# A transposed-map pair of the second group takes one of the scores' two PSUM banks

## The chip, the core and the metric

The kernel runs on one core of a Trainium2 chip. The metric is the device time of one execution in microseconds. The profile shows one execution of the program; its times are from the profiled span's start, and the engines are PE (TensorE matmul; its weight loads are a row of their own, PEld), DVE (VectorE), ACT (ScalarE) and SP, which here only issues DMAs.

## What is computed

One layer on a sequence of 1024 tokens of width 2048, in float32. An adaptive norm, one input projection, then two mixers side by side and one output projection with residual and final norm:

```
proj = hn @ w_in
# group A: 8 heads; two softmax maps per head, subtracted, chunk-causal over blocks of 128 queries
p = softmax(where(mask, q k^T * scale, -inf));  a = p[:, 0] - lam * p[:, 1];  o = a @ v
# group B: 4 heads; a state per chunk of 64 tokens
state = decay * state + k_dec^T @ v;  o = q @ state
mixed = concat([rmsnorm(o_A) * silu(dg), rmsnorm(o_B) * silu(gg)]) @ w_out
out = rmsnorm(x + gate * mixed)
```

## The kernel before

Tokens are worked on in two halves of 512. Every large product runs as three matmuls on a high and a low part of its operands (lines 189 to 192 and 218 to 220), so PE has 11118 matmuls. A `unit` (line 821) is a quarter of a half: two attention heads h0 and h1 and one gated-linear head. In the program's order a unit has: the projections dk, dq, dg of h0, the projection of v for both heads (`make_v`, line 605), attention of h0, the projections of h1, attention of h1, then gq, two gg and gv, and `gla` (line 773). The second half has the same four units with twice the keys, and the output projection of the first half follows (lines 1007 to 1056).

The engines' instructions are not issued in the program's order. A planner simulates the program and lets each engine take, of what is ready, what comes first in the program's order. What it decides is fixed: at run time every engine works through its list in that order. So while attention waits for a softmax, PE's list holds matmuls of a projection that comes later in the program; below these are called filler.

PSUM has eight banks of 128x512 fp32. Three pools hold them: `pj_p` has four, for projections (`pb`, `pa`); `sc_p` has two, for the scores `s` of attention (line 663) and the two state products `kv` of a gla step (line 785); `ms_p` has two, for the transposed maps `tp` (line 700), the attention output `av` (line 696), the sums of the norm `nps` (line 624), the gla output `o` (line 802) and some small things.

Attention of a head works on two groups of two query blocks. For each block there are two maps, each of one piece (first half) or two pieces (second half: `ka`, the 512 keys of the first half, and `kb`). A piece is scored into a bank of `sc_p`, its maximum is taken on DVE (line 669), and ACT writes the exponentials to a buffer `p` (line 678; six buffers). The two maps are then subtracted (line 693). When a group's two blocks are done, the maps are transposed, two key blocks at a time, into a `tp` tile (line 708), split into a high part on ACT and a low part on DVE (`aT`, line 711, two buffers) and multiplied with v into `av` (lines 720 to 722). The second group has two `tp` tiles per head in the first half and four in the second half. `av` keeps its bank of `ms_p` through its group, so the `tp` tiles of the group take the other bank in turn.

In `gla`, a step t multiplies `kd_z` and `gv` into two `kv` banks (line 788), adds them to the state `S` on DVE (line 796, two buffers), splits the state (`sr`, one buffer) and multiplies it with gq into `o` (line 804). `gv` shares the three `vb` buffers with the v of two heads (lines 606 and 877).

Of the kernel before, what the change touches and what calls it, by code (L numbers as in the profile page):

```python
# [10 lines left out]
F32 = mybir.dt.float32  # L11
# [8 lines left out]
P = 128  # L20
# [3 lines left out]
TOK = 512  # L24
# [71 lines left out]
def body(ctx, tc, A, out):  # L96
# [13 lines left out]
    sc_p = ctx.enter_context(tc.tile_pool(name="sc", bufs=2, space=PSUM))  # L110
    ms_p = ctx.enter_context(tc.tile_pool(name="ms", bufs=2, space=PSUM))
# [116 lines left out]
    def split(hi, lo, src, lo_eng=None):  # L228
        SC.copy(hi, src)
        (lo_eng or V).tensor_tensor(lo, src, hi.bitcast(F32), ALU.subtract)  # L230
# [412 lines left out]
    def attention(half, h, qt, kb, vb, g_t):  # L643
# [8 lines left out]
        for grp in range(2):  # L652
# [44 lines left out]
            nk = nka + 2 * grp + 2  # L697
            for k0 in range(0, nk, 2):
                last = k0 == nk - 2
                tp = ms_p.tile([P, TOK], F32, name=f"tp{half}{h}{grp}{k0}", tag="ms")  # L700
                pi, ko = (0, k0) if k0 < nka else (half, k0 - nka)
                spans = []
                o = 0
                for k in (0, 1):
                    for bi in range(2):
                        if last and k == 1 and bi == 0:
                            continue
                        PE.transpose(tp[:, o:o + P], at[bi][pi][:, (ko + k) * P:(ko + k + 1) * P], ident)
                        o += P
                aT = hd_p.tile([P, 2, TOK], F32R, name=f"aT{half}{h}{grp}{k0}", tag="aT", bufs=2)  # L710
                split(aT[:, 0, :o], aT[:, 1, :o], tp[:, :o])
                for k in (0, 1):
                    vv, kt = (va, k0 + k) if k0 < nka else (vb, ko + k)
                    vh, vl = vv[:, kt, 0, :], vv[:, kt, 1, :]
                    if last and k == 1:
                        dst, sl = av[:, P:2 * P], slice(2 * P, 3 * P)
                    else:
                        dst, sl = av[:, :2 * P], slice(k * 2 * P, (k + 1) * 2 * P)
                    first = k0 == 0 and k == 0
                    PE.matmul(dst, vh, aT[:, 0, sl], start=first, stop=False, skip_group_check=True)  # L720
                    PE.matmul(dst, vh, aT[:, 1, sl], start=False, stop=False, skip_group_check=True)
                    PE.matmul(dst, vl, aT[:, 0, sl], start=False, stop=last and k == 1, skip_group_check=True)
# [98 lines left out]
    def unit(half, g, first, kdec):  # L821
# [23 lines left out]
        g0 = gate_tile(h0)  # L845
        vt = make_v(dv_ps if first else proj_a(A["wina"][A_AT[("dv", g)]], hn), half, g)
        attention(half, h0, qt0, kb0, vt[0], g0)
        kb1 = make_k(src("dk", h1), half, h1)
        qt1 = make_q(src("dq", h1), half, h1)
        g1 = gate_tile(h1)  # L850
        attention(half, h1, qt1, kb1, vt[1], g1)
        if g == 0:
            kdec = gla_p.tile([P, 4, 512], F32, name=f"kdec{half}", tag="kdec")
# [254 lines left out]
```

## Time and profile before

| | before |
|---|---|
| median of 3 runs | 1957.07 us (1956.12 to 1958.6) |
| the profiled execution | 1955.52 us |
| its span | 1953.7 us |
| PE busy in the span | 1905.5 us (98%) |
| DVE, ACT busy | 1321.9 us, 968.7 us |
| mean granted TensorE clock | 0.987 of 2.4 GHz |

The span runs from the first to the last instruction; 1.8 us of the execution's time lie around it. Matmuls overlap, and a matmul's duration in a row is longer than the distance to the next one's start, so the time a run of matmuls takes is read from starts. A bracket at the end of a timeline row gives the idle time of that engine just before the instruction, and which instruction ended it.

### The profile page before, as it was taken

How to read it: one execution, taken by the hardware profiler on the slowest of the kernel's cores; microseconds unless marked ns; L12 is line 12 of the kernel's file. 1: busy time of each engine (PE TensorE's matmuls, PEld its weight loads, DVE VectorE, ACT ScalarE, POOL GpSimd, SP SyncE). 2: the span in 40 equal slices, each digit the busy share in tenths (PEclk: the TensorE clock that was granted, in tenths of full speed). 3: DMA queues.
4: the chain of work that ended last, by engine and by line, in shares of the span. 5: the costliest groups of instructions: out<-in, count | busy, mean ns of one | idle time of the engine just before them, and what ended most of it. 6: DMA issues, size and time to landing. Idle time of an engine off the chain costs nothing.

```text
span 1953.7 us, 28965 instructions
## 1 busy us (share of the span) xinstructions
PE 1905.5 (98%) x11118; PEld 1677.0 (86%) x11118; DVE 1321.9 (68%) x2496; ACT 968.7 (50%) x1811; POOL 0.7 (0%) x6
## 2 busy tenths in 40 slices
PE   7999999999989999999999999999999999899998
PEld 4888999899868989889899898989888998688888
DVE  7897876577779767656676666866785675534444
ACT  4222865566545566545545555554654544323323
POOL 0000000000000000000000000000000000000000
PEclk9899999999999999999999999999999999799999
DMA  9884434332665444433344323533263723466543
GB/s 362 294 290 136 155 125 141 119 106 87 209 210 166 136 138 150 135 89 101 97 154 117 106 91 108 162 111 99 87 198 117 267 86 106 167 239 213 162 150 120
DMA packets 111758, 298.16 MB, mean 153 GB/s; under 512 B 11098, under 2 KB 31322, under 8 KB 111108
## 3 DMA queue, kind: packets, MB, share of 16 engines
q1 hardware_dynamic: 111620, 296.32, 46.6%
q8 instruction: 87, 1.43, 0.3%
q14 instruction: 51, 0.42, 0.1%
HBM read 258.00 MB, written 38.28 MB: 152 GB/s over the span
## 4 chain that ended last, share of the span: by engine, by line
PE 86%; DMA 6%; DVE 6%; issue 1%; ACT 1%; SPq 0%; DVEq 0%; ACTq 0%
PE pa L218 8%; PE pa L220 8%; PE pa L219 8%; PE pa L1051 4%; PE pa L1052 4%; PE pa L1053 4%; PE pb_dk L190 2%; PE pb_dk L191 2%; PE pb_dk L192 2%; PE pb_gg L190 2%; PE pb_dg L191 2%; PE pb_dq L192 2%; PE pb_dq L191 2%; PE pb_dq L190 2%; PE pb_dg L192 2%; PE pb_gg L192 2%
## 5 line engine op out<-in xcount | busy, mean ns | idle before, releaser
L180 DVE TENSOR_TENSOR w<-wr,w 128x1024 fp32r<-128x1024 f32 (+1 forms) x294 | 352.1, 1198 | 276.0 <-ACT w L179 274.8
L179 ACT CAST w<-wr 128x1024 fp32r<-128x1024 f32 (+1 forms) x294 | 303.2, 1031 | 431.2 <-PE pa L1053 116.1
L220 PE MATMUL pa<-w,hn 128*128 128x256 f32 (+1 forms) x1152 | 328.2, 285 | 0.0
L218 PE MATMUL pa<-w,hn 128*128 128x256 f32 (+1 forms) x1152 | 327.7, 285 | 0.0
L219 PE MATMUL pa<-w,hn 128*128 128x256 f32 (+1 forms) x1152 | 327.7, 285 | 0.0
L219 PEld LDWEIGHTS pa<-w,hn 128*128 128x128 f32 x1152 | 219.6, 191 | 2.4 <-issue 0.2
L218 PEld LDWEIGHTS pa<-w,hn 128*128 128x128 f32 x1152 | 219.5, 191 | 2.3 <-issue 0.5
L220 PEld LDWEIGHTS pa<-w,hn 128*128 128x128 f32 x1152 | 219.5, 191 | 1.5 <-issue 0.2
L678 ACT ACTIVATE p<-s,sm 128x512 f32<-128x512 f32 (+2 forms) x192 | 110.7, 580 | 130.1 <-DVE sm L675 59.0
L1051 PE MATMUL pa<-w,mx 128*128 128x512 f32 x384 | 150.7, 392 | 0.4 <-DVE h L996 0.4
L1052 PE MATMUL pa<-w,mx 128*128 128x512 f32 x384 | 150.4, 392 | 0.0
L1053 PE MATMUL pa<-w,mx 128*128 128x512 f32 x384 | 149.9, 392 | 0.0
L669 DVE TENSOR_REDUCE sm<-s 128x1 f32<-128x512 f32 (+2 forms) x192 | 105.5, 551 | 46.7 <-PE s L666 44.1
L190 PE MATMUL pb_gg<-hn,w 128*128 128x512 f32 x224 | 88.1, 394 | 0.6 <-DVE vb L230 0.6
L191 PE MATMUL pb_dk<-hn,w 128*128 128x512 f32 x224 | 88.1, 393 | 0.0
L190 PE MATMUL pb_dk<-hn,w 128*128 128x512 f32 x224 | 88.1, 393 | 0.0
L190 PE MATMUL pb_dg<-hn,w 128*128 128x512 f32 x224 | 88.1, 393 | 0.0
L191 PE MATMUL pb_gg<-hn,w 128*128 128x512 f32 x224 | 88.0, 393 | 0.0
L192 PE MATMUL pb_dq<-hn,w 128*128 128x512 f32 x224 | 87.9, 392 | 0.0
L191 PE MATMUL pb_dg<-hn,w 128*128 128x512 f32 x224 | 87.8, 392 | 0.0
L192 PE MATMUL pb_gg<-hn,w 128*128 128x512 f32 x224 | 87.8, 392 | 0.0
L192 PE MATMUL pb_dk<-hn,w 128*128 128x512 f32 x224 | 87.6, 391 | 0.0
(394 smaller groups left out, 4376.9 us busy)
## 6 DMA issues: line engine op xcount, KB each, us to landing
wr<-in_winb SPq DMA_DIRECT2D x142, 512.0 KB, 3.8
wr<-in_wina SPq DMA_DIRECT2D x72, 512.0 KB, 3.8
wr<-in_wout SPq DMA_DIRECT2D x64, 512.0 KB, 3.5
ada<-in_wada SPq DMA_DIRECT2D x44, 512.0 KB, 5.0
stage<-in_wgate SPq DMA_DIRECT2D x64, 256.0 KB, 3.0
mx<-mixd SPq DMA_DIRECT2D x32, 512.0 KB, 8.1
ada_kdec<-in_wada SPq DMA_DIRECT2D x20, 512.0 KB, 6.6
mixd<-wr_d SPq DMA_DIRECT2D x16, 512.0 KB, 4.5
```

The source lines that it names most:

```text
L179: paced = SC.copy(w[:, 0, :n], raw[:, :n])
L180: (lo_eng or V).tensor_tensor(w[:, 1, :n], raw[:, :n], w[:, 0, :n].bitcast(F32), ALU.subtract)
L190: PE.matmul(ps, w_hi, h[:, 0, :], start=first, stop=False)
L191: PE.matmul(ps, w_hi, h[:, 1, :], start=False, stop=False)
L192: PE.matmul(ps, w_lo, h[:, 0, :], start=False, stop=last)
L218: PE.matmul(o, ah, wh, start=st, stop=False, skip_group_check=True)
L219: PE.matmul(o, ah, wl, start=False, stop=False, skip_group_check=True)
L220: PE.matmul(o, al, wh, start=False, stop=kt == KT - 1, skip_group_check=True)
L678: SC.activation(p_[:, :n], pss[pi][:, :n], AF.Exp, bias=nm, scale=0.125, accum_out=sm[:, 4 + 2 * m_ + pi:5 + 2 * m_ + pi])
L1051: PE.matmul(pss[t_], ah, wh, start=kt == 0, stop=False)
L1052: PE.matmul(pss[t_], ah, wl, start=False, stop=False)
L1053: PE.matmul(pss[t_], al, wh, start=False, stop=kt == KT - 1)
```

## The change

The `tp` tiles of a head's second group (`grp` is 1) come from `sc_p` with its tag instead of `ms_p`. The first group's stay where they were. No instruction is added or removed; 48 of the 80 `tp` tiles have another bank.

```diff
-                tp = ms_p.tile([P, TOK], F32, name=f"tp{half}{h}{grp}{k0}", tag="ms")
+                tp = (sc_p if grp else ms_p).tile([P, TOK], F32, name=f"tp{half}{h}{grp}{k0}", tag="sc" if grp else "ms")
```

## Rows read from the trace of the kernel before

**Rows 1.** The page's part 1: busy time, share of span, instructions.

```profile
PE 1905.5 (98%) x11118; PEld 1677.0 (86%) x11118; DVE 1321.9 (68%) x2496; ACT 968.7 (50%) x1811; POOL 0.7 (0%) x6
```

**Rows 2.** Stretches: us, PE, PEld, DVE, ACT, POOL busy (count), clock, DMA share, GB/s.

```profile
1450.00:1500.00 50.00, 48.01 (x239) 40.23 (x238) 30.01 (x51) 23.46 (x40) 0.00 (x0) 1.00 0.40 124
1500.00:1550.00 50.00, 46.51 (x331) 44.56 (x330) 34.98 (x76) 28.27 (x61) 0.00 (x0) 0.93 0.72 266
...
1650.00:1700.00 50.00, 39.88 (x156) 29.98 (x156) 35.49 (x68) 21.54 (x55) 0.00 (x0) 0.80 0.50 173
```

**Rows 3.** Waits of PE: us in total, times, longest.

```profile
PE s L665 <- ACT p L678: 4.6, 5, 1.9
...
PE av L720 <- ACT aT L229: 2.9, 2, 2.6
```

**Rows 4.** The tile aT: durations min/median/max ns, first and last start, forms.

```profile
L229 ACT CAST aT<-tp x80: 455/577/651, 233.6 to 1659.9; 128x512 fp32r<-128x512 f32 x48, 128x384 fp32r<-128x384 f32 x32
L230 DVE TENSOR_TENSOR aT<-tp,aT x80: 494/676/693, 234.1 to 1661.3; 128x512 fp32r<-128x512 f32 x48, 128x384 fp32r<-128x384 f32 x32
```

**Rows 5.** Timeline of PE, the last head's second group: start, us, instruction.

```profile
1643.50 0.60 PE L708 MATMUL tp<-ident,p 128*128 128x128 f32 x4
...
1650.30 0.60 PE L708 MATMUL tp<-ident,p 128*128 128x128 f32 x4
...
1657.28 0.49 PE L708 MATMUL tp<-ident,p 128*128 128x128 f32 x3
1660.39 0.38 PE L720 MATMUL av<-aT,vb 128*128 128x256 f32 x1 [2.63 <-ACT aT L229]
```

**Rows 6.** Timeline of DVE and PE around norm sums, first and last head end.

```profile
272.31 0.39 PE L628 MATMUL nps_d<-wr_d,ones 128*128 128x512 f32 x1
272.55 0.49 PE L708 MATMUL tp<-ident,p 128*128 128x128 f32 x3
...
1635.75 0.69 DVE L230 TENSOR_TENSOR sr<-S,sr 128x512 fp32r<-128x512 f32 x1 [0.69 <-ACT sr L229]
...
1665.09 0.80 PE L628 MATMUL nps_d<-wr_d,ones 128*128 128x512 f32 x1 [1.84 <-ACT wr_d L229]
1665.68 1.48 PE L804 MATMUL o<-sr,gq 128*128 128x512 f32 x3
```

**Rows 7.** Timeline of PE, end of one head, first scores of the next.

```profile
1559.83 0.40 PE L665 MATMUL s<-ka,qt 128*128 128x512 f32 x1
...
1566.49 0.40 PE L665 MATMUL s<-ka,qt 128*128 128x512 f32 x1
...
1571.24 0.49 PE L708 MATMUL tp<-ident,p 128*128 128x128 f32 x3
...
1587.58 0.49 PE L708 MATMUL tp<-ident,p 128*128 128x128 f32 x3
```

**Rows 8.** Timeline of PE and ACT, state products before the last unit's v.

```profile
1457.24 0.88 PE L788 MATMUL kv<-gv,kd_z 128*128 128x256 f32 x6
...
1474.35 0.39 PE L192 MATMUL pb_gq<-hn,w 128*128 128x512 f32 x1
...
1476.01 0.60 PE L788 MATMUL kv<-gv,kd_z 128*128 128x256 f32 x3
1476.77 0.66 ACT L229 CAST vb<-pa 128x256 fp32r<-128x256 f32 x2
1479.03 0.49 PE L708 MATMUL tp<-ident,p 128*128 128x128 f32 x3
1480.17 0.50 PE L190 MATMUL pb_gg<-hn,w 128*128 128x512 f32 x1 [0.65 <-DVE vb L230]
```

**Rows 9.** Timeline of PE and DVE at the end of attention.

```profile
1655.65 0.39 PE L1053 MATMUL pa<-w,mx 128*128 128x512 f32 x1
...
1677.12 1.88 DVE L996 TENSOR_TENSOR h<-pa,gbs 128x512 f32<-128x512 f32 x3
1677.86 0.80 PE L1051 MATMUL pa<-w,mx 128*128 128x512 f32 x1 [0.45 <-DVE h L996]
```

## The prediction

> **What bounds the kernel now.** The page's part 1 comes first. PE is busy 1905.5 of 1953.7 us [rows 1], so all of PE's idle time is 48.2 us, and a change that adds and removes no instruction can win at most that, plus time lost at the lower clock level. Then the stretches, 50 us each, to see where the idle time lies. A good part of it is outside attention (the start, the last stores). What the change can touch is in three stretches of the second half [rows 2]: 2.0 us (50 less 48.01) in 1450:1500, 3.5 us in 1500:1550 and 10.1 us in 1650:1700, where the granted clock is also 0.80. Everywhere else in the second half's attention filler covers the waits: PE waited 2.9 us in all for a split map and 4.6 us in all for an exponential to leave a scores' bank [rows 3]. So attention's length matters only through what runs out of filler. The timelines tell which: in 1650:1700 the filler's last matmul is at 1655.65 and the next is at 1677.86, after DVE has emptied a bank [rows 9]; around 1475 the last gq matmul is at 1474.35, and the next projection waits until 1480.17 for DVE's split of v [rows 8].
>
> **Banks are handed out in the program's order.** This is the reading on which my forecast rests. The step-0 state of the last gla is split by 1636.4 (1635.75 and 0.69), yet the `o` made from it starts at 1665.68, right behind `nps` of the last head at 1665.09; in the first head, the next head's first transposes start at 272.55, right behind `nps` at 272.31 [rows 6]. Both are users of `ms_p` that come later in the program than `nps`, and one bank of the pool had been free for some time. I take it that a pool's tiles get their banks in the program's order, whoever is ready first. Then putting `tp` in `sc_p` also puts it in that pool's line, ahead of the next head's scores and of `kv`.
>
> **What it removes.** In the second group, `tp` of one pair waits until ACT and DVE have read the pair before it. The two splits are 0.58 and 0.68 us [rows 4], but in PE's list a pair comes every 6.9 us in the last head ((1657.28 less 1643.50)/2) [rows 5], and every 5.45 us in the even head before it ((1587.58 less 1571.24)/3) [rows 7]. With two banks the first two pairs go together and the last two go one release later: one pitch where there were three. That saves two pitches, 10.9 to 13.8 us, of a head's latency in the second half; with two pairs a head, in the first half, one pitch. On PE itself it saves at most the 2.9 us of rows 3. The bound below is zero: the pitch is far longer than the splits, so part of it is the planner's order and need not fall. I take the pitch to be the bank's release as the planner sees it, since pairs follow each other so evenly, and book the full two pitches.
>
> **First added wait: the next head's scores.** In the even head of the last unit, the last scores start at 1559.83, the first full `tp` at 1571.24; the odd head's first scores go between them, at 1566.49 [rows 7]. In the program's order they now need the banks of the third and fourth pair: 1571.24 and two releases of 5.45, so 1582.1, 15.6 us later. Behind these scores wait DVE's maximum, the exponentials and so on, that is, all of the odd head. How much of 15.6 is felt at that head's end? Its first group's transposes were themselves waiting for `nps` of the even head [rows 6], which now comes 10.9 earlier, and its own second group gives back 10.9 to 13.8. The end of the odd head so moves between 13.8 us earlier (nothing is felt) and 4.7 us later (15.6 less 10.9, all is felt). The middle is 4.6 earlier, and I take 5 earlier.
>
> **Second added wait: kv.** In the third unit of the second half the first `kv` goes at 1457.24, in the middle of the odd head's second group, 21.8 us before the group's last `tp` at 1479.03; the last goes at 1476.01, and 0.8 us later ACT begins to split the last unit's v, since `gv` has let go of the `vb` buffers [rows 8]. That split empties projection banks, and PE's next projection starts 4.16 us after the last `kv`. Under the change `kv` comes behind the last `tp`: 1474.0 (5 earlier), one release of 5.45, then the same 18.8 us from first to last `kv`, which is 1498.2; with 4.16 the filler begins again at 1502.4 instead of 1480.17. That is 22.2 us later, between 13.4 (odd head's end 13.8 earlier) and 31.9 (4.7 later). What is queued behind on PE is the rest of the projections and the whole output projection. In the three other units nothing stands so close: I book zero for them, because projections there have other banks to go on with; if that cover is gone too, it is one more unit at a few us.
>
> **Where that time goes.** The filler that starts late also ends late, and so it covers the idle time that follows. Between 1480.17 and 1677.86 PE idles 13.6 us (3.5 and 10.1) [rows 2]; I let all of it be covered. The norm sum and first `o` move ahead of the restart, 0.80 and 1.48 us [rows 6], which is 2. The lower clock now sits in 1650:1700 and would sit in 1475:1502 instead, so I book zero for it. At a mean of 0.80 over 50 us, 20 us are at the lower level (1.2 of 2.4 GHz), 10.1 of them idle; the other 10 cost 5 us. That is the bound on both sides. The sum: 22.2 - 13.6 - 2 = 6.6 us slower. Against the profiled execution's 1955.52 us that is 1962.1; the median of the runs is 1.55 us above that execution, so the forecast is **1963.7 us**. Its ends: 13.4 - 13.6 - 2 = -2.2, about 1955; and 31.9 - 10.1 with the 3.5 us stall staying, +21.8, about 1979.
>
> **Rivals.** *Faster: the shorter chain wins.* If banks go to whoever is ready, or the odd head's scores were early for nothing, each second group is two pitches shorter and nothing waits behind it. The last head then ends 13.8 us earlier, while filler still runs to 1655.65, and the idle 10.1 us of 1650:1700 shrink, with up to 5 us of clock: 5 to 15 us, so 1942 to 1952, say 1948. For it: the pairs in rows 5 stand in a line, and PE ran dry just at the last of them. Against it: the order in rows 6. The Trainium skill has the rule for this rival, in "Perfetto Trace Analysis", section "Matmuls": independent groups of matmuls should take turns among PSUM banks, so that emptying one bank goes on beside the next group's matmuls. By that rule the change is right and the time falls to this rival's. The trace agrees that emptying and transposing don't overlap before, and it also shows a bank taken from another user, of which the rule says nothing.
>
> *No change: the waits cancel.* If the odd head ends some 9 to 14 us earlier, the restart of the filler moves by 13 to 18 us and the idle time behind it takes 15.6 of that: 1957 within 4 us. For it: PE's work is the same, and attention in the first half is covered by filler throughout.
>
> *The change doesn't do what it says.* If the pitch of `tp` is not the bank's but the list's (splits take 1.25 us, pairs come every 5.45 to 6.9), nothing is saved, `kv` and scores still stand in line, and the odd head ends later by up to the 15.6 us: about 1975.
>
> **How the numbers follow.** About 0.2% (4 us) is what a measurement of this kernel can tell from no change. Chances: the forecast 0.38, faster 0.24, no change 0.30, the pitch that stays 0.08. Slower by over 0.2% is the forecast and the last, 0.46; same 0.30; faster 0.24. The range goes from the upper part of the faster rival to the upper part of the forecast, 1947 to 1977; the rest of both lies outside, about 2 in 10.
>
> **What would show it.** Right: in the second half an odd head's first scores start after the even head's last `tp`; `tp` comes in two pairs with one pitch between; all `kv` follow the odd head's last `tp`; a new idle stretch of 15 us or more on PE near 1475:1502, ended by the split of v, with a granted clock below 1.00; and less than 10.1 us idle around 1650:1700. Wrong: scores of the next head still ahead of `tp` (then the order of banks is not the program's), no idle stretch at the last unit's v (then another bank let the filler go on), or a `tp` pitch as before. The prediction would also be wrong by some us if the planner's new order made DVE's in-order waits for DMAs fall elsewhere, which no row here prices.

## The result, and the profile after

| | before | after |
|---|---|---|
| median, runs taken together | 1956.89 us (4 runs) | 1975.03 us (4 runs) |
| ratio, with 95% interval | | 1.0098 (1.0087 to 1.0110) |
| the profiled execution | 1955.52 us | 1975.19 us |
| its span | 1953.7 us | 1973.1 us |
| PE busy in the span | 1905.5 us | 1916.5 us |
| mean granted TensorE clock | 0.987 | 0.982 |

The change costs 1.0%. The page's part 1 of the kernel after, against [rows 1]:

```profile
PE 1916.5 (97%) x11118; PEld 1681.8 (85%) x11118; DVE 1318.4 (67%) x2496; ACT 968.6 (49%) x1811; POOL 0.7 (0%) x6
```

The instructions are the same. Of the 19.4 us by which the span grew, 8.4 are idle time of PE (1973.1 less 1916.5 is 56.6, against 48.2) and 11.0 are busy time of the same 11118 matmuls. Part of the 11.0 is the lower clock: PE was busy at the lower of its two levels for 36.5 us before and 51.1 us after, which at half speed is 7.3 us more.

Where it happens is read from a longer stretch of 200 us, by the number of matmuls that PE got done. The kernel before (columns as in [rows 2]):

```profile
1300.00:1500.00 200.00, 198.01 (x1140) 173.84 (x1139) 140.08 (x268) 108.93 (x208) 0.00 (x0) 1.00 0.41 125
```

The kernel after:

```profile
1300.00:1500.00 200.00, 187.86 (x1066) 162.67 (x1066) 137.06 (x267) 106.11 (x206) 0.00 (x0) 0.97 0.35 112
```

Most of the loss is here: 74 matmuls fewer in 200 us. At the 5.7 a us of before (1140 in 200) that is 13 us, roughly, since the matmuls are not of one size. Up to 1100, 17 are missing (6417 for 6434). The three stretches of [rows 2], in the kernel after:

```profile
1450.00:1500.00 50.00, 40.57 (x201) 32.99 (x199) 31.43 (x60) 25.87 (x50) 0.00 (x0) 0.90 0.29 93
1500.00:1550.00 50.00, 47.52 (x274) 40.82 (x275) 38.75 (x85) 29.05 (x63) 0.00 (x0) 1.00 0.52 177
...
1650.00:1700.00 50.00, 40.23 (x174) 30.48 (x173) 33.30 (x71) 21.94 (x53) 0.00 (x0) 0.82 0.30 98
```

A new hole of 9.4 us (50 less 40.57) stands in 1450:1500, with a granted clock of 0.90; the old hole in 1650:1700 is still 9.8 us (10.1 before) at 0.82. The first did not fill the second.

The timeline of PE in the kernel after, last unit: the even head's last scores, its second group's transposes, the odd head's first scores; then the last head's scores and transposes, `kv`, `nps`, and the output projection's restart. It answers [rows 5], [rows 6], [rows 7] and [rows 9]:

```profile
1571.95 0.40 PE L665 MATMUL s<-ka,qt 128*128 128x512 f32 x1
...
1589.21 0.93 PE L708 MATMUL tp<-ident,p 128*128 128x128 f32 x7
...
1594.81 0.44 PE L665 MATMUL s<-ka,qt 128*128 128x512 f32 x1
...
1649.45 0.40 PE L665 MATMUL s<-ka,qt 128*128 128x512 f32 x1
...
1657.19 0.27 PE L708 MATMUL tp<-ident,p 128*128 128x128 f32 x1
...
1657.99 0.27 PE L708 MATMUL tp<-ident,p 128*128 128x128 f32 x1
...
1660.87 0.82 PE L708 MATMUL tp<-ident,p 128*128 128x128 f32 x6
...
1668.18 0.93 PE L708 MATMUL tp<-ident,p 128*128 128x128 f32 x7
...
1673.89 0.28 PE L788 MATMUL kv<-gv,kd_z 128*128 128x256 f32 x1
...
1677.07 0.40 PE L628 MATMUL nps_d<-wr_d,ones 128*128 128x512 f32 x1
...
1696.66 0.80 PE L1051 MATMUL pa<-w,mx 128*128 128x512 f32 x1 [1.71 <-DVE h L996]
```

Two pairs start 0.8 us apart (1657.19, 1657.99), and their other six transposes go together at 1660.87. The third and fourth pair come as one block of seven transposes, 7.3 us behind these six: one pitch where there were three. The odd head's scores stand behind that block (1594.81, against 1566.49 before), and `kv` behind the last head's block (1673.89). The projection restarts at 1696.66, 18.8 us later than before (1677.86): nearly all of the 19.4 us lies ahead of that point.

The hole itself, on PE in the kernel after:

```profile
1468.67 0.39 PE L192 MATMUL pb_dg<-hn,w 128*128 128x512 f32 x1
...
1477.01 0.48 PE L708 MATMUL tp<-ident,p 128*128 128x128 f32 x1 [4.46 <-ACT p L678]
...
1480.76 0.79 PE L190 MATMUL pb_gq<-hn,w 128*128 128x512 f32 x1 [2.61 <-DVE rt_q L579]
...
1482.21 0.63 PE L190 MATMUL pb_gq<-hn,w 128*128 128x512 f32 x1
1482.64 0.63 PE L191 MATMUL pb_gq<-hn,w 128*128 128x512 f32 x1
...
1495.82 0.40 PE L192 MATMUL pb_gq<-hn,w 128*128 128x512 f32 x1
...
1509.42 0.39 PE L190 MATMUL pb_gg<-hn,w 128*128 128x512 f32 x1
1509.65 0.39 PE L191 MATMUL pb_gg<-hn,w 128*128 128x512 f32 x1
```

and on ACT beside it:

```profile
1472.35 0.62 ACT L600 CAST qt<-rt_q 64x512 fp32r<-64x512 f32 x1 [0.59 <-PE s L665]
...
1476.18 0.69 ACT L678 ACTIVATE p<-s,sm 128x512 f32<-128x512 f32 x1
...
1477.65 2.34 ACT L578 COPY rt_q<-pb_dq 32x512 f32<-32x512 f32 x4
1480.01 0.60 ACT L240 ACTIVATE gt<-pb_dg 128x512 f32<-128x512 f32 x1
...
1506.85 0.65 ACT L229 CAST vb<-pa 128x256 fp32r<-128x256 f32 x2
```

The filler ends at 1468.67 and goes on at 1480.76: its four banks hold the last unit's v (read from 1498.76 on and again at 1506.85), a finished dq (read at 1477.65) and a finished dg (first read at 1480.01). In between PE has only attention, and waits for exponentials; on ACT these (1476.18) stand behind the copies of q and k that start at 1472.35. After the hole the matmuls start 0.43 us apart (1482.21, 1482.64), where two at 1509 are 0.23 apart: the granted clock stood at the lower level, 1.2 of 2.4 GHz.

This is not the only stop of the filler. Behind gq it stops again, from 1495.82 to 1509.42, and in the second unit it had stopped behind gq from 1295.89 to 1309.45; both of these end when v has been split behind the last `kv`, as the prediction had it for one unit. The three stops (columns as in [rows 2]):

```profile
1295.89:1309.45 13.56, 10.15 (x51) 7.20 (x50) 13.00 (x27) 9.26 (x21) 0.00 (x0) 1.00 0.21 73
1468.67:1480.76 12.09, 3.44 (x14) 1.80 (x12) 7.39 (x17) 10.86 (x22) 0.00 (x0) 0.70 0.22 87
1495.82:1509.42 13.60, 10.34 (x52) 7.15 (x50) 13.25 (x27) 9.38 (x21) 0.00 (x0) 1.00 0.25 77
```

PE does 117 matmuls in these 39.25 us, where 5.7 a us would be 224. The kernel before has two shorter stops within the second half's attention, 1474.35 to 1480.17 [rows 8] and 1531.99 to 1538.12, and none in the second unit.

### The profile page after: what moved, and what is told of

Same layout as the page of the kernel before. It is cut to its first block, busy times and chain, and to the rows that moved or that the text cites. A ratio compares the mean times of both kernels' runs of the same rounds, so it can differ in the third digit from the quotient of the medians.

```text
span 1973.1 us, 28972 instructions
## 1 busy us (share of the span) xinstructions
PE 1916.5 (97%) x11118; PEld 1681.8 (85%) x11118; DVE 1318.4 (67%) x2496; ACT 968.6 (49%) x1811; POOL 0.7 (0%) x6
## 4 chain that ended last, share of the span: by engine, by line
PE 87%; DVE 6%; DMA 5%; ACT 1%; issue 1%; SPq 0%; DVEq 0%; ACTq 0%
PE pa L220 8%; PE pa L218 8%; PE pa L219 8%; PE pa L1051 4%; PE pa L1053 4%; PE pa L1052 4%; PE pb_dk L191 2%; PE pb_dk L190 2%; PE pb_dk L192 2%; PE pb_gg L190 2%; PE pb_gg L191 2%; PE pb_gg L192 2%; PE pb_dq L192 2%; PE pb_dg L190 2%; PE pb_dg L192 2%; PE pb_dq L191 2%
## 5 line engine op out<-in xcount | busy, mean ns | idle before, releaser
L191 PE MATMUL pb_dk<-hn,w 128*128 128x512 f32 x224 | 88.5, 395 | 0.0
L192 PE MATMUL pb_dq<-hn,w 128*128 128x512 f32 x224 | 88.5, 395 | 0.0
L190 PE MATMUL pb_dk<-hn,w 128*128 128x512 f32 x224 | 88.4, 395 | 0.0
L190 PE MATMUL pb_dq<-hn,w 128*128 128x512 f32 x224 | 87.7, 392 | 0.0
```

The source lines that it names most:

```text
L190: PE.matmul(ps, w_hi, h[:, 0, :], start=first, stop=False)
L191: PE.matmul(ps, w_hi, h[:, 1, :], start=False, stop=False)
L192: PE.matmul(ps, w_lo, h[:, 0, :], start=False, stop=last)
```

## The experiments

One table holds what the traces of the second half say of each kernel. "Tail" is the time from the start of a head's last map's scores to the start of its last transpose, mean over four even or four odd heads; "gap" is the time from the even head's last map's scores to the odd head's first scores, mean over four units. All three are differences of starts on PE's timeline, such as 1668.84 (the seventh transpose of the block at 1668.18) less 1649.45 for the last tail of the kernel after.

| kernel | tail, even | tail, odd | gap | ratio to before (95%) |
|---|---|---|---|---|
| before | 30.4 | 34.1 | 7.8 | 1 |
| the change | 20.5 | 21.7 | 26.1 | 1.0098 (1.0087 to 1.0110) |
| even heads alone | 21.2 | 28.2 | 25.9 | 1.0154 (1.0135 to 1.0172) |
| odd heads alone | 30.7 | 21.7 | 7.1 | 0.9905 (0.9890 to 0.9920) |
| scores wait, no bank moved | 27.5 | 28.8 | 27.6 | 1.0292 (1.0276 to 1.0309) |
| kv waits, no bank moved | 30.7 | 33.2 | 8.2 | 1.0002 (0.9992 to 1.0011) |
| odd heads, and one pair of the even | 24.2 | 21.1 | 7.7 | 1.0006 (0.9995 to 1.0018) |
| one pair of the odd heads | 30.1 | 27.9 | 7.4 | 0.9979 (0.9969 to 0.9989) |

**Even heads alone.**

```diff
+                on_sc = grp == 1 and h % 2 == 0
+                tp = (sc_p if on_sc else ms_p).tile([P, TOK], F32, name=f"tp{half}{h}{grp}{k0}", tag="sc" if on_sc else "ms")
```

> Only the even heads' second groups take the scores' banks; odd heads' stay with the output. Theory of the line (banks go in the program's order): the first scores of the odd heads still come behind the even head's last transposed pair (from 1566 to about 1590 in the last unit), but the state products of gla are ahead of the odd head's transposes as before, so projections start again near 1480 and the gla steps of the last unit lie before 1660 again. The odd head's end is then later by the 10 to 15 us of the scores less what its first group gets back; expected 1957 plus 5 to 12 us, 1962 to 1969. Rival (two transposed pairs at a time crowd ACT and DVE, whichever heads): half of the 18 us, about 1966, with the odd head's scores as early as before. Rival (the planner's order is merely reshuffled): anything within 1950 to 1975, with no such pattern in the starts.

1982.93 us, 1.0154: slower than the whole change, and than the 1962 to 1969 that I expected. The even head's tail shrinks by 9.2 us, but the gap to the odd head grows by 18.1.

**Odd heads alone.** The same edit with `h % 2 == 1`.

> Only the odd heads' second groups take the scores' banks. Theory of the line: the odd heads' first scores come before the even head's last transposes again (near 1566 in the last unit), the odd head's four pairs take one pitch instead of three, but all state products of gla still come behind them. In the last unit the gla steps so lie behind attention's end, and the output projection's third column starts again 5 to 10 us later than 1677.9; expected 1959 to 1968. If the two waits simply add, this and the run with the even heads together make the 18 us. Rival (crowding of ACT and DVE): about 1966, state products no matter.

1933.75 us, 0.9905: faster than before and than the change, where I expected 1959 to 1968. The three stretches of [rows 2] in this kernel:

```profile
1450.00:1500.00 50.00, 50.00 (x245) 42.13 (x244) 38.13 (x72) 27.54 (x54) 0.00 (x0) 1.00 0.39 122
1500.00:1550.00 50.00, 50.00 (x396) 48.89 (x395) 31.51 (x70) 29.86 (x60) 0.00 (x0) 1.00 0.77 281
...
1650.00:1700.00 50.00, 48.15 (x202) 38.12 (x201) 26.84 (x46) 15.72 (x31) 0.00 (x0) 0.93 0.53 180
```

In these stretches 1.85 us are idle, of the 15.6 of [rows 2]; another 2.5 lie in 1600:1650, where the kernel before has none. Its PE timeline, last head:

```profile
1625.02 0.93 PE L709 MATMUL tp<-ident,p 128*128 128x128 f32 x7
...
1632.38 0.92 PE L789 MATMUL kv<-gv,kd_z 128*128 128x256 f32 x6
...
1638.62 0.40 PE L628 MATMUL nps_d<-wr_d,ones 128*128 128x512 f32 x1
```

`kv` stands behind the last `tp` here too, and the head's end, `nps` at 1638.62, comes 26.5 us earlier than in [rows 6]: the kernel gains in spite of the second wait. The two halves of the change have opposite signs and don't simply add: +1.54 and -0.95 make +0.59%, the whole is +0.98.

**The whole change but for the last head.** `on_sc = grp == 1 and not (half == 1 and h == 7)`.

> The change as it is, but for the last head of the second half, whose second group stays with the output. Theory of the line: in the last unit the state products go during the last head's transposes again (they were at 1633 to 1650 before the change, 1674 to 1688 after it), so the steps of gla no longer lie as a row of waits behind attention; the last head has three pitches of 6.9 again, which is 13.8 us lost. The stretch between the last filler and the restart of the output projection shrinks from some 23 us by the gla steps, about 10 us: 1965 to 1976, and if the tail is where most of the loss sits, the lower end. Rival (the loss sits in the idle stretches at 1296 and 1496 alone): 1975, no gain.

1972.88 us, 1.0108 (1.0092 to 1.0125). With the last `kv` chain released from the wait nothing comes back. This run alone doesn't show that the loss isn't made at the end, because the last head has its long tail again (28.6 us, 19.4 in the change) and the two could cancel; the stops of the filler above show where it is made.

**Another user on the scores' banks.** The kernel before, with the gla output `o` in `sc_p`; `tp` stays.

```diff
-            o = ms_p.tile([P, 2, 256], F32, name=f"o{half}{g}{t_}", tag="ms")
+            o = sc_p.tile([P, 2, 256], F32, name=f"o{half}{g}{t_}", tag="sc")
```

> The kernel before, with one other edit: the outputs of the gla steps come from the scores' banks instead of the output's; transposed maps are all where they were before. Theory of the line: before, these outputs stand behind the norm sum of the odd head, for which their pool's banks are kept; in the scores' line they come right behind the state products, so in the last unit they go between 1637 and 1657 instead of 1665.7 to 1677, the next unit's scores start some 5 to 8 us earlier, and the idle 10 us near 1660 shrink: 1945 to 1955. Rival (banks go to whoever is ready, and the outputs waited for something else): outputs still start behind the norm sum, 1957 within 4 us.

1965.61 us, 1.0073 (1.0053 to 1.0092). Its PE timeline, last unit:

```profile
1647.40 0.39 PE L804 MATMUL o<-sr,gq 128*128 128x512 f32 x1
...
1674.28 0.39 PE L628 MATMUL nps_d<-wr_d,ones 128*128 128x512 f32 x1
```

Out of the line of `ms_p`, the first `o` goes 27 us ahead of `nps`; in [rows 6] it went right behind it. That is the reading of the bank order: `o` had waited only for its turn. The time still rose, where I expected 1945 to 1955. Most of the loss is made ahead of the second half's first scores, which start at 851.96 instead of 841.3; that the scores' line got longer by `o` would explain it, but no run takes it apart.

**The first wait alone.** The kernel before, with the odd head's first score matmul issued only after the even head's last transpose.

```diff
+                        if h % 2 and b == m_ == pi == 0:
+                            with tc.issue_after(last_tp[0].ins):
+                                PE.matmul(ps_[:, :n], qt[:, m_, qs], kk[:, m_, :n], start=True, stop=False)
...
+                        last_tp[0] = PE.transpose(tp[:, o:o + P], at[bi][pi][:, (ko + k) * P:(ko + k + 1) * P], ident)
```

> The kernel before, with one order added: in each unit the odd head's first score matmul is issued only after the even head's last transpose. No bank is moved, so this is the first added wait alone. Theory: this wait is what costs the time in the change; then this kernel is as slow as the one with the even heads' move alone or slower, since nothing is given back by a shorter second group: +20 to +45 us, 1.0 to 2.3%. Rival: the loss comes from crowding the scores' banks with more tiles, not from the order; then this kernel stays within 4 us of before.

2010.87 us, 1.0292: slower as the theory said, and by more than its 1.0 to 2.3%. Its PE timeline:

```profile
1294.97 2.60 PE L794 MATMUL kv<-gv,kd_z 128*128 128x256 f32 x9 [6.50 <-ACT p L684]
...
1421.25 0.58 PE L218 MATMUL pa<-w,hn 128*128 128x256 f32 x1 [8.73 <-DVE rt_q L579]
...
1636.63 0.49 PE L714 MATMUL tp<-ident,p 128*128 128x128 f32 x3
1636.88 0.48 PE L669 MATMUL s<-ka,qt 128*128 128x512 f32 x1
```

The scores go right behind the last transpose (1636.63, 1636.88), and the same two kinds of hole open as in the change: PE waits for exponentials, and the filler for `rt_q`. The gap is the same 26 to 28 us as in the change and in the even heads' move, without any bank moved; and shorter tails give back less (some 3 us in the even heads and 5 in the odd, against 10 and 12 in the change), which fits that it is the slowest.

**The second wait alone.** The kernel before, with the first `kv` of each gla issued only after the odd head's last transpose.

```diff
+                    if t_ == n == 0:
+                        with tc.issue_after(last_tp[0].ins):
+                            PE.matmul(kv[i][:, :256], kd_z[:, a, i, t_, :], gv[b][:, t_, :], start=n == 0, stop=n == 2)
```

> The kernel before, with the other order added: in each unit the first state product (the first kv matmul of step 0) is issued only after the odd head's last transpose. No bank is moved, so this is the second added wait alone. My prediction booked +22.2 us at the restart of the filler for it, less what idle time behind it takes: that is +5 to +15 us here, since no head gets shorter. Rival, from the run in which the odd heads alone were moved, where kv also comes behind the last transpose and the time fell: the order of kv alone costs nothing, within 4 us of before.

1954.30 us, 1.0002 (0.9992 to 1.0011): nothing, as the rival said, though the wait is there, as its PE timeline shows:

```profile
1652.23 0.49 PE L710 MATMUL tp<-ident,p 128*128 128x128 f32 x3
1652.48 0.48 PE L792 MATMUL kv<-gv,kd_z 128*128 128x256 f32 x2
...
1676.22 0.80 PE L1057 MATMUL pa<-w,mx 128*128 128x512 f32 x1 [4.27 <-DVE h L1002]
```

The last unit's first `kv` is at 1652.48 instead of 1633.4, and the output projection restarts at 1676.22, 1.6 us earlier than in [rows 9]. In the third unit the projections stand still from 1472.99 to 1488.54 (1474.35 to 1480.17 before), yet PE idles less in 1450:1550 than before, 3.8 us against 5.5, at a full clock:

```profile
1450.00:1500.00 50.00, 46.24 (x222) 37.00 (x221) 34.67 (x60) 25.98 (x48) 0.00 (x0) 1.00 0.39 122
1500.00:1550.00 50.00, 50.00 (x361) 47.35 (x360) 32.79 (x74) 28.48 (x58) 0.00 (x0) 1.00 0.74 273
```

So the idle time behind the late restart did cover it, as the prediction had reasoned for its sum.

**By halves.** Odd heads of the second half alone (`grp == 1 and h % 2 == 1 and half == 1`), and the whole change in the first half alone (`grp == 1 and half == 0`).

> Only the odd heads of the second half have their second group's tiles on the scores' banks. Theory: the gain of the odd heads' move is made in the second half, where PE runs dry behind attention; then the time is that of all odd heads moved, 0.990 to 0.992 of before (about 17 us less). Rival: half of it or more comes from the first half, where odd heads that end earlier start the second half earlier; then 0.995 or more.

> The change in the first half only, in even and odd heads. Theory: filler covers attention there, the loss is made in the second half; within 4 us of before. Rival: the first half's order, too, sets when the second half's units start (before, the first one starts at 841.3, in the changed kernel at 843.9), and the time lost there is kept: +4 to +10 us.

1937.77 us, 0.9912 (0.9897 to 0.9927), and 1956.53 us, 1.0012 (1.0002 to 1.0021). The gain is made in the second half. So is the loss, but for some 2 us; this is by difference, since no run has the change in the second half alone.

**How much of the line.** Odd heads as above, and of the even heads the second pair alone (`grp == 1 and (h % 2 == 1 or k0 == 2)`); then the second pair of the odd heads alone (`grp == 1 and h % 2 == 1 and k0 == 2`).

> Odd heads: all tiles of the second group on the scores' banks. Even heads: the second pair alone (k0 = 2), the others on the old banks. So the next head's scores stand behind one tile that is let go of soon after the group's first transposes, not behind the third and fourth. Theory: the loss grows with how long the odd head's scores are held back; their first pieces start some 5 to 10 us later than before (20 to 28 in the change), and the time lies between the odd heads' move alone and the change: 0.994 to 1.004 of before. Rival 1: one tile in the line costs as much as all, since it holds its bank from the moment the even head's last scores are read; then 1.008 or more. Rival 2: one tile early enough costs nothing and the even heads' shorter group pays; then below 0.990.

> Only the second pair (k0 = 2) of the odd heads' second groups is on the scores' banks; the other tiles stay. Theory: the gain of the odd heads' move is the saved pitches; here one of the two is saved (first and second pair go together, the third and fourth still take turns on one bank), so about half of the gain: 0.994 to 0.997. Rival: the gain is that kv stands behind the odd head's transposes, or that the old banks are less crowded, so one tile does the whole: 0.992 or less. If pitches don't matter at all: 0.999 to 1.001.

The first: 1954.61 us, 1.0006, between the odd heads' move and the change. The time is in the theory's range, but not by its way, since the odd heads' first pieces start no later. One tile in the line takes all of the 0.95% back, although the gap is 7.7, as before: the first piece gets a bank, the next ones wait, and the odd heads' scores then take 73 us from first to last (mean of 63.1, 81.7, 80.8 and 66.2), against 62.5 before. The second: 1950.10 us, 0.9979. I expected half of the gain for one of two pitches and measured about a quarter: the odd tail fell by 6.2 of the 12.4 us, but time doesn't follow it in proportion.

**What holds the filler.** From the rows of the hole I took it that an odd head's last scores set how far the filler reaches, since `qt` has one buffer: the next q can't be written before, `rope` keeps its buffer, and a bank stays full. Two kernels hold the next q (and k) back on ACT until the odd head's last map is split, with nothing else moved.

```diff
+            if half and h and h % 2 == 0 and m_ == 0:
+                with tc.issue_after(last_cast[0].ins):
+                    SC.copy(qt[a, m_, :], r_[a, :])
```

> The kernel before, with one order added on ACT, in the second half: the q of a unit's even head is written to the one buffer qt only after the last map of the odd head before it has been split, instead of right after that head's last scores. No bank is moved and no score, transpose or kv is made to wait for another; the new q itself is needed only 20 us after that point. Theory: the filler can run no further than the four banks of the projections, and the one that holds the next q is emptied only when the last head's scores are through with qt; so filler runs dry about 20 to 35 us in each unit, and the kernel is 15 to 60 us slower (0.8 to 3%), though attention's own order is as before. Rival: the filler has other banks to go on with, and only attention's own chain counts; within 4 us of before.

1952.68 us, 0.9991 (0.9982 to 1.0001): the theory fell. But only the first of the four copies into `qt` was held. So the second kernel holds them all, and the next odd head's `kb` too:

```diff
+    def held(half, on, h):
+        return tc.issue_after(casts[h].ins) if half and on and h > 0 else nullcontext()
...
+            with held(half, h % 2 == 1, h - 2):
+                SC.copy(kb[a, m_, :], r_[a, :])
...
+            with held(half, h % 2 == 0, h - 1):
+                SC.copy(qt[a, m_, :], r_[a, :])
+                SC.copy(qt[b, m_, :], r_[a, :])
```

> The kernel before, with orders added on ACT in the second half: all four copies into qt of a unit's even head, and both copies into kb of the odd head that follows it, wait until the last map of the odd head before them has been split; before, they go right behind that head's last scores. So both rope buffers stay full some 35 us longer, and with them two of the four projection banks; the two of v are let go of by the kv chain as before. No score, transpose or kv is made to wait, and the new q and k are needed only some 20 us later. Theory: last scores set the filler's reach; with all four banks held the filler runs dry some 15 us in each of three units: 10 to 45 us slower, 0.5 to 2.3%. Rival, as with one copy of q alone held: there is always a bank to go on with; within 4 us of before.

1945.95 us, 0.9964 (0.9949 to 0.9978): faster, where I expected at least 10 us slower. The hold is real. ACT's timeline in this kernel:

```profile
1468.85 0.62 ACT L607 CAST qt<-rt_q 64x512 fp32r<-64x512 f32 x1
...
1472.70 2.34 ACT L578 COPY rt_q<-pb_dq 32x512 f32<-32x512 f32 x4
```

The q is written at 1468.85 instead of 1442.48, and dq is read 9.7 us after the last dg matmul (1463.04), against 9.0 in the change; yet PE is busy 47.96 of 50 us in 1450:1500, because `kv` is over at 1464.70, v leaves its banks, and gq starts in one of them at 1468.90. Late q and k alone stop the filler only from 1463.04 to 1468.90, and a late `kv` alone stops it at no cost (above). In the change both were late at once, and all four banks were full. That the two together open the hole fits these three traces, but no run did both without the late scores, so it is argued and not shown. And the other two banks need not be those of v. In the kernel with the first wait alone the filler stops for 8.73 us, until 1421.25, with no `kv` made to wait: two banks hold dq and dg there, and two hold `gv`, whose low parts DVE reads only behind the even head's end (its last transposes are at 1437.47):

```profile
1440.49 1.29 DVE L230 TENSOR_TENSOR gv<-pa,gv 128x512 fp32r<-128x512 f32 x2 [0.19 <-PE av L728]
```

In the even heads' move alone the stop ahead of gq opens twice (1276.27 to 1288.59 and 1472.21 to 1487.92), with `kv` behind no transpose: there the odd head's last scores are late (1477.64), and both the next q (1479.30) and, in the scores' own pool, `kv` (1483.96) come behind them. Late scores are what these stops have in common.

Why the hold gains 0.36% is suggested by ACT's rows, and no run took it by itself. The odd tails fell from 34.1 to 31.3. The exponentials of the last map of the third unit's odd head, first in the kernel before, then in this one:

```profile
1452.78 0.69 ACT L678 ACTIVATE p<-s,sm 128x512 f32<-128x512 f32 x1
...
1441.43 0.69 ACT L685 ACTIVATE p<-s,sm 128x512 f32<-128x512 f32 x1
```

Before, they start 12.1 us behind the scores (1440.69), with the copies of q, k and dq between them on ACT; with the hold it is 6.2 us (1435.26), and this head's tail falls from 38.6 to 32.7.

## Why the prediction was right, and where not

The forecast was slower, 1963.7 us within 1947 to 1977; measured were 1975.0. The sign, the order of the waits and the range hold. The size does not, and 1975.0 is near the end of the range: the sum gave +6.6, and the profiled executions differ by 19.7 (1975.19 less 1955.52).

**Banks in the program's order: right.** Odd heads' scores and all `kv` stand behind the last `tp`, and `o` jumps 27 us ahead when it leaves the pool's line. This decided against the rival in which banks go to whoever is ready.

**The removed wait: right in size.** Two pitches, 10.9 to 13.8 us, were booked for a head. The tails fell by 9.9 (even) and 12.4 (odd).

**The first added wait: mis-sized, and the heaviest term.** +15.6 us were booked for the odd head's first scores; the gap grew by 18.3 (26.1 less 7.8). Then I took the middle of -13.8 and +4.7 for the odd head's end, 5 us earlier. From the even head's last scores to the odd head's last `tp` it is 104.4 us before and 109.1 after (means of the four units): 4.7 later, the end at which all of the wait is felt. The shorter tail gave back 12.4 of the 18.3 and little else came back: the odd head's scores take 61.3 us from first to last (62.5 before). So the even head's `nps` had not set the odd head's length, as I had reasoned for the middle. The run with this wait alone costs 2.9%, with no bank moved: it is what makes the change slower.

**The second added wait: right in order, wrong in price.** The filler's restart was put at 1502.4, up to 1512.1 by the bounds, and is at 1509.42. But I let the whole 22.2 us count as a loss, to be covered by idle time behind it. The wait alone costs nothing: the projections stand still for 15.6 us in that run, and the idle time behind takes it back. In the change the filler stops three times ahead of attention's end. The stop from 1468.67 to 1480.76 is ended by the reading of dq, and the prediction did not have it; the two that v's split ends are of the predicted kind, one of them in a unit that was booked at zero. How much of these two is the order of `kv` and how much the late odd head ahead of it, no run separates; where the odd head is early (odd heads alone), the order costs nothing.

**The idle time behind: wrong.** All 13.6 us were to be covered. The two stretches lost 1.3 of it (2.5 and 9.8 us are left). The last unit is as dry as before because attention ended later together with the filler: `nps` by 12.0 us (1677.07 against 1665.09), the filler's last matmul ahead of the restart by 16.4 (1672.84 against 1656.46; the 1655.65 of the prediction is not the last one).

**The clock at zero: right in the sum, wrong in the place.** The low clock was to move from 1650:1700 to the new hole. It is in both (0.82 and 0.90), and gone from 1500:1550 (1.00, before 0.93). From 1100 on PE is busy at the lower level for 21.1 us, before for 19.9. The 5 us that bounded this term were too few: of the 20.5 us at the lower level around 1650:1700, 14.0 were busy, not 10. **Zero for the other units: wrong.** The second unit's filler stops for 13.6 us.

Most of these errors pull one way. With the end of the odd head at its bound and the stall staying, the prediction's own upper end was +21.8 (19.8 with the 2 us of `nps` and `o`, which it leaves out there), and about that came. This is luck in part: that end lets a late `kv` cost the time and 10.1 us of idle time cover some of it, while late scores cost it and 1.3 us were covered.

**Rivals.** "The pitch doesn't change" named 1975 us for a wrong reason: the pitch did change. "No change" needed an odd head that ends 9 to 14 us earlier, and it ends later. "Faster" was right for half of the heads. The Trainium skill, in "Perfetto Trace Analysis", section "Matmuls", advises that independent groups take turns among PSUM banks; the traces agree for the odd heads (tails 12.4 us shorter, 0.9905) and not for the even ones (1.0154), where the bank taken was one that the next head was about to use.

**The better kernel** is the odd heads' move alone: 0.9905 of before (0.9890 to 0.9920), some 18 us less.

## What to carry to other kernels

Where a pool's banks go round in the program's order, moving a tile into another pool also puts it ahead of everything that comes later there: look at who is next in that line before the tile's own gain is counted. The same move paid where the next user was a state product with time to spare, and cost where it was the next head's scores, the start of a long chain. Price a wait by what stands behind it with no cover, not by how late it makes one instruction: here `kv` moved 19 us in the last unit at no cost, while scores moved 20 us for 2.9%.

## What was not expected of the hardware

After the hole at 1470 to 1481, matmuls start 0.43 us apart instead of 0.23, until the clock is granted in full again. Yet most of what the change lost to the lower clock does not lie behind a hole that it opened. Of the 14.6 us more that PE is busy at the lower level, 10.2 lie in 550:600 of the first half, where PE idles no more than before. Before and after:

```profile
550.00:600.00 50.00, 42.31 (x254) 35.99 (x255) 39.40 (x98) 24.90 (x51) 0.00 (x0) 1.00 0.67 207
...
550.00:600.00 50.00, 42.95 (x225) 37.29 (x224) 38.33 (x78) 22.78 (x43) 0.00 (x0) 0.90 0.62 195
```

Why the clock fell there in one kernel and not in the other, these traces don't show. The rest of the 11.0 us of longer busy time, some 3.7, is not taken apart; a matmul that stands alone in a stop counts with its whole row, 0.40 us, and one in a run with the 0.23 us to the next one's start.
